# A two-block network on one core: another order of the expert units with late products last, and less GpSimd arithmetic behind the experts

## The chip, the cores and the metric

The kernel runs on one core of a Trainium2 chip. The metric is the device time of one execution in microseconds (us); less is better. The core has five engines that run their own instruction streams in order and meet at semaphores: PE (TensorE, the matmuls), DVE (VectorE), ACT (ScalarE), POOL (GpSimd) and SP (SyncE, which here only issues DMAs). DMAs are also issued from POOL's stream.

## The reference, cut to what matters

Everything is float32; `x` is 512 tokens of 1024 values, `c` one row of 1024.

```python
# block 1: a mixer, then 4 of 32 experts for each token
h = rmsnorm(x, norm2_w) * (1 + scale2) + shift2
gates = softmax(top4(h @ w_router + b_router))
hu = h[rows of e] @ w_up[e] + b_up[e]              # 1024 -> 2 x 1024
glu, lin = minimum(hu[:, :1024], 7), clip(hu[:, 1024:], -7, 7)
y = (glu * sigmoid(1.702 * glu) * (lin + 1)) @ w_down[e] + b_down[e]
x = x + gate2 * (sum over the 4 experts of gates * y)
# block 2: four sublayers: windowed attention, MLP, recurrent block, MLP
shift, scale, gate = split(silu(c) @ ada_w[i, s] + ada_b[i, s])
x = layer_norm(sqrt2 * x + (1 + gate) * f(x * (1 + scale) + shift), ln_g, ln_b)
```

An expert's weights are 8 MB for the up half and 4 MB for the down half; all 32 experts are read, 384 MB.

## The kernel before, in words

**Expert stage** (about 430 to 1528 us of the span). Experts are ranked by their number of tokens, and the table `UNITS` (L37-48) lays the ranks out as 20 blocks of 128 rows in 10 units: `_single(a)` is a block that one expert fills, `_pair(a, b, n)` one that two experts share. A unit is a list of steps, a step a list of blocks (mostly one). For every unit the tokens of its blocks are gathered by matmuls with one-hot columns (`gather_T`, L1145; `gather_unit` always makes 256 columns). For every step `expert_up` runs the up half (`bank_hu`, 8 tiles of 1 MB for each expert), then `expert_down` runs the down half of the step **before** it (`bank_y`, 4 tiles for each expert), and `transposed` (L1203) turns the new activations round. All products go through `products` (L1134). `pin` holds PE to the order in which the code is written. Rank 2 and on are known only on the chip: SP loads the expert's number into a register (L1277) before it can issue that expert's weights.

The weights come through a ring of 13 buffers of 1 MB, filled by SP in the order of use (L301); a load waits for its buffer. After unit 1 (`LOOP`) stands a loop for overflowing experts, which makes no trip on this input.

The result of a block is scaled by its tokens' gates on ACT (`expert_out`) and scattered by an indirect DMA of POOL (L1226) to `y_d` in DRAM, which has four slots for each token. In the last unit, behind its first step, `expert_bias` adds the bias term, and `add_slots` (L1447-1459) reads the four slots of all tokens back: 16 loads of 512 KB issued by POOL (L1456) into three pairs of buffers, each pair added, multiplied by `g2bc` (the second gate, spread over the partitions) and added to `x` on DVE. The last two blocks never go through `y_d`: `late_add` scales them (L1246), splits them in a high and a low part (L1247, L1248), multiplies both by the transposed one-hot rows `hotT` on PE (L1251, L1252) and adds the bank to `x` on DVE (L1253). The first late block's `late_add` stands ahead of the transposes and of the last down half in PE's order.

**Stages behind the experts** (1528 to 2862 us). Matmuls are made of three passes over parts that are split in high and low (`mm3`, L319-321); the weights come as 512 KB tiles and are split by ACT (`wh`, L310) and by DVE or POOL (`wl`, L315 or L313). `add_y` multiplies a result by the gate (L1618, DVE) and adds it to `x` (L1619, mostly POOL). `stats` and `normalise` (L1625-1633, DVE) make the layer norm, with small 128x1 steps for the root (L326-338); `make_hT` transposes `x` on PE (L1596), and ACT and DVE split it (`h_hi`, `h_lo`, L1603). `affine` (L1643, L1644, POOL) then multiplies `x` by `ln_g` and adds `ln_b`, for the residual. The modulation rows come from `c` times `ada_w`: three of them inside attention, `ada(1, ...)`, by `gemv_split`: for each of 8 tiles a multiply and add over 128x1024 on ACT, DVE (L389) or POOL (L392) into `gacc`, and 4 matmuls at the end (L395). `behind(3)` places instructions behind the last `h_hi` and `h_lo` of `make_hT`.

Of the kernel before, what the change touches and what calls it, by code (L numbers as in the profile page):

```python
# [256 lines left out]
def tile_block(ctx, tc, A, out, dbg=None):  # L257
# [118 lines left out]
    def gemv_split(src, cofs, gp, ring_raw, nv=4):  # L376

        acc = gp.tile([128, 1024], F, tag="gacc", name="gacc", bufs=1)
        for k in range(KD):
            if ring_raw:  # L380
                r = raw(src[k])
            else:
                r = gp.tile([128, 1024], F, tag="graw", name="graw", bufs=2)
# [721 lines left out]
    hot0 = [hot_cols(Z[:, :, 64 + b], hot_of(b, (b, 0, 128, 0))) for b in range(2)]  # L1105
# [46 lines left out]
    def gather_unit():  # L1152
        return gather_T([hots[-1][:, tb] for tb in range(NTB)], 256)
# [76 lines left out]
    def late_rows(b):  # L1230

        hotT = mt([128, 1024], "ma", 3, FR, mo)[:, 0:512]
        pt = trbank()
        for tb in range(NTB):
            pin(pe.matmul(out=pt[:, tbs[tb]], lhsT=hots[-1][:, tb, 128 * b:128 * b + 128].bitcast(F), rhs=ident,
                          start=True, stop=True))
        act.copy(out=hotT, in_=pt)
        return hotT

    def late_add(y, gc, hotT):  # L1240

        yh, yl = (mt([128, 8, 128], "aT", 3, FR, mo).rearrange("p a b -> p (a b)") for _ in range(2))
        t_ = mt([128, 1024], "yb", 2, F, mo)
        for h in range(2):
# [3 lines left out]
            vec.tensor_tensor(out=yl[:, hs], in0=t_[:, hs], in1=yh.bitcast(F)[:, hs], op=OP.subtract)  # L1248
            for tb in range(NTB):
                o = pbank("hu")  # L1250
                pin(pe.matmul(out=o, lhsT=hotT[:, tbs[tb]], rhs=yh[:, hs], start=True, stop=False))  # L1251
                pin(pe.matmul(out=o, lhsT=hotT[:, tbs[tb]], rhs=yl[:, hs], start=False, stop=True))  # L1252
                vec.tensor_tensor(out=xs[tb][:, hs], in0=o, in1=xs[tb][:, hs], op=OP.add)  # L1253
# [193 lines left out]
    def add_slots():  # L1447

        spare = mt([128, 8, 256], "xT", 2).rearrange("p a b -> p (a b)")
        pairs_ = [[h2_("l", 0), h2_("l", 1)], [h2_("l", 2), h2_("l", 3)], [spare[:, 0:1024], spare[:, 1024:2048]]]  # L1450
        for tb in range(NTB):
            for j in (0, 2):
                y = pairs_[0]
                pairs_.append(pairs_.pop(0))
                for i, t in enumerate(y):
                    pool.dma_start(out=t, in_=y_d[(j + i) * T + tb * 128:(j + i) * T + tb * 128 + 128, :])  # L1456
                vec.tensor_tensor(out=y[0], in0=y[0], in1=y[1], op=OP.add)
# [579 lines left out]
```

## Time and profile before

| | before |
|---|---|
| median of 3 runs | 2861.84 us (2855.33 to 2865.29) |
| profiled execution | 2863.78 us, span 2861.8 us |
| mean granted TensorE clock | 0.96 |
| PE, DVE, ACT, POOL busy | 92%, 50%, 27%, 17% of the span |
| DMA | 647.34 MB, mean 226 GB/s |
| slices 9 to 20 of 40 (572 to 1431 us) | 370 to 422 GB/s |
| chain that ended last | PE 46%, DMA 15%, DVE 12%, ACT 2% |

The times of the profile count from the span's start. A row of a group of instructions ends with the idle time of its engine just before them and what ended most of it; a row of a timeline has that in brackets. In a row of windows the DMA share can stand a little above 1.

### The profile page before, as it was taken

The page shows a single profiled execution, that of the slowest core. Times are in us where ns is not written, and L with a number is a line of the kernel's source. Part 1 is how long each engine was busy: PE and PEld are TensorE (multiplying, and loading weights), DVE is VectorE, ACT ScalarE, POOL GpSimd, SP SyncE. Part 2 cuts the span into 40 slices and gives each one's busy share as a digit, 9 for nine tenths or more (in the row PEclk, how much of TensorE's full clock was granted, in tenths as well). Part 3 has the DMA queues.
Part 4 walks back from the last instruction along what each step waited for, and adds up shares of the span by engine and source line. Part 5 has one row for each costly group of instructions (what it writes and reads, how often), then busy time and mean ns, then how long its engine had stood idle before and what let it go on. Part 6 is the DMA issues. An engine that isn't in the chain of part 4 may idle for free.

```text
span 2861.8 us, 37210 instructions
## 1 busy us (share of the span) xinstructions
PE 2620.6 (92%) x14592; PEld 1705.2 (60%) x14592; DVE 1419.4 (50%) x2470; ACT 766.5 (27%) x1312; POOL 483.3 (17%) x371
## 2 busy tenths in 40 slices
PE   7999998988999999999948898999988898799997
PEld 4777774433445334334315567777867677688886
DVE  4865573211112111111254668676478888855456
ACT  4432430000000100001004444232235555333231
POOL 1000000000000000000013213333251334422223
PEclk9999998999999999999978998999999899799999
DMA  7355457799999999999983424564323222232231
GB/s 269 111 178 185 149 184 291 306 421 389 421 421 372 422 421 421 421 421 370 421 346 130 157 81 151 175 225 150 98 77 105 72 86 86 70 107 95 89 103 52
DMA packets 128241, 647.34 MB, mean 226 GB/s; under 512 B 16272, under 2 KB 17252, under 8 KB 78912
## 3 DMA queue, kind: packets, MB, share of 16 engines
q1 hardware_dynamic: 121936, 628.07, 57.9%
q0 software_dynamic: 5984, 16.35, 1.5%
q8 instruction: 116, 1.90, 0.3%
q14 instruction: 61, 0.50, 0.1%
q10 hardware_dynamic: 144, 0.52, 0.0%
HBM read 624.42 MB, written 22.12 MB: 226 GB/s over the span
## 4 chain that ended last, share of the span: by engine, by line
PE 46%; DMA 15%; DVE 12%; ACT 2%; issue 2%; POOL 0%; DVEq 0%; SPq 0%; ACTq 0%
PE bank_hu L1134 11%; DMA raw<-in_w_up_dram 6%; PE bank_y L1134 5%; PE bank_d L319 5%; PE bank_d L321 4%; PE bank_d L320 4%; DMA raw<-in_w_down_dram 4%; PE bank_u L321 3%; PE bank_u L319 3%; PE bank_u L320 3%; DVE wl L315 2%; DMA graw<-in_ada_w_dram 2%; PE bank_tr L1145 2%; DMA raw<-in_ada_w_dram 1%; DVE vv L1951 1%
## 5 line engine op out<-in xcount | busy, mean ns | idle before, releaser
L1134 PE MATMUL bank_hu<-raw,xT 128*32 128x512 f32 (+2 forms) x3456 | 573.5, 598 | 13.7 <-DMA raw<-in_w_up_dram 13.7
L1134 PEld LDWEIGHTS bank_hu<-raw,xT 128*32 128x32 f32 (+2 forms) x3456 | 203.2, 124 | 363.1 <-issue 323.6
L315 DVE TENSOR_TENSOR wl<-raw,wh 128x1024 fp32r<-128x1024 f32 (+1 forms) x222 | 315.7, 1431 | 124.7 <-ACT wh L310 123.1
L310 ACT CAST wh<-raw 128x1024 fp32r<-128x1024 f32 (+1 forms) x231 | 236.6, 1042 | 442.6 <-PE bank_u L320 169.9
L1619 POOL TENSOR_TENSOR h2h<-h2h,yt 128x512 f32<-128x512 f32 x161 | 238.2, 1487 | 686.3 <-DVE yt L1618 676.4
L1134 PE MATMUL bank_y<-raw,aT 128*32 128x512 f32 (+2 forms) x1536 | 259.7, 596 | 8.9 <-DMA raw<-in_w_down_dram 8.8
L1191 DVE TENSOR_SCALAR ma<-bank_hu 128x256 f32<-128x256 f32 x80 | 34.0, 425 | 468.2 <-PE bank_hu L1134 468.2
L319 PE MATMUL bank_u<-h_hi,wh 128*128 128x512 f32 (+1 forms) x680 | 253.7, 375 | 5.9 <-ACT h_hi L1603 3.1
L321 PE MATMUL bank_u<-h_hi,wl 128*128 128x512 f32 (+1 forms) x680 | 253.0, 373 | 6.2 <-DVE wl L315 6.2
L320 PE MATMUL bank_u<-h_lo,wh 128*128 128x512 f32 (+1 forms) x680 | 252.6, 372 | 5.8 <-DVE h_lo L1603 5.8
L319 PE MATMUL bank_d<-wh,a 128*128 128x512 f32 x512 | 202.5, 396 | 5.7 <-DVE yt L1618 3.4
L1618 DVE TENSOR_TENSOR yt<-bank_d,G 128x512 f32<-128x512 f32 x168 | 113.2, 686 | 182.9 <-PE bank_d L321 177.2
L320 PE MATMUL bank_d<-wl,a 128*128 128x512 f32 x512 | 200.6, 392 | 0.0
L1192 ACT ACTIVATE mb<-ma 128x256 f32<-128x256 f32 x80 | 33.3, 417 | 619.0 <-DVE ma L1191 612.9
L321 PE MATMUL bank_d<-wh,b 128*128 128x512 f32 x512 | 197.7, 393 | 0.0
L1134 PEld LDWEIGHTS bank_y<-raw,aT 128*32 128x32 f32 (+2 forms) x1536 | 84.3, 124 | 173.2 <-issue 155.4
L1226 POOL DMA_INDIRECT y_d<-yb,ii x18 | 17.7, 984 | 921.0 <-ACT yb L1223 689.7
L321 PEld LDWEIGHTS bank_u<-h_hi,wl 128*128 128x128 f32 x680 | 132.2, 195 | 29.3 <-DVE wl L315 7.0
L320 PEld LDWEIGHTS bank_u<-h_lo,wh 128*128 128x128 f32 x680 | 132.4, 195 | 28.3 <-DVE h_lo L1603 6.4
L319 PEld LDWEIGHTS bank_u<-h_hi,wh 128*128 128x128 f32 x680 | 132.3, 196 | 27.8 <-ACT h_hi L1603 3.3
L1204 DVE COPY aT<-bank_tr 128x512 f32<-128x512 f32 x20 | 13.8, 691 | 246.2 <-PE bank_tr L1203 246.2
L319 PEld LDWEIGHTS bank_d<-wh,a 128*128 128x128 f32 x512 | 96.4, 188 | 31.1 <-DVE yt L1618 5.6
(556 smaller groups left out, 4264.0 us busy)
## 6 DMA issues: line engine op xcount, KB each, us to landing
raw<-in_w_up_dram SPq DMA_DIRECT2D x256, 1024.0 KB, 19.3
raw<-in_w_down_dram SPq DMA_DIRECT2D x128, 1024.0 KB, 19.8
raw<-in_mlp_w_dram SPq DMA_DIRECT2D x128, 512.0 KB, 4.4
graw<-in_ada_w_dram SPq DMA_DIRECT2D x72, 512.0 KB, 4.1
graw<-in_w_ada_dram SPq DMA_DIRECT2D x48, 512.0 KB, 4.7
raw<-in_ada_w_dram SPq DMA_DIRECT2D x24, 512.0 KB, 3.6
raw<-in_rnn_w_in_dram SPq DMA_DIRECT2D x24, 512.0 KB, 4.0
raw<-in_w_in_dram SPq DMA_DIRECT2D x22, 512.0 KB, 4.0
```

The source lines that it names most:

```text
L310: act.copy(out=h, in_=r)
L315: vec.tensor_tensor(out=l, in0=r, in1=h.bitcast(F), op=OP.subtract)
L319: pe.matmul(out=o, lhsT=lhs[0], rhs=rhs[0], start=first, stop=False)
L320: pe.matmul(out=o, lhsT=lhs[0], rhs=rhs[1], start=False, stop=False)
L321: pe.matmul(out=o, lhsT=lhs[1], rhs=rhs[0], start=False, stop=last)
L1134: pin(pe.matmul(out=o[at + a:at + a + tile], lhsT=lhs[:, a:a + tile], rhs=rhs, start=start, stop=stop, tile_position=(0, at + a)))
L1145: pin(pe.matmul(out=pt[:, j * n:j * n + n], rhs=hot[tb], lhsT=h2s[part][tb][:, (k + j) * 128:(k + j + 1) * 128], start=part + tb == 0, sto ...
L1191: vec.tensor_scalar(out=a, in0=hu[:, 0:256], scalar1=7.0, scalar2=None, op0=OP.min)
L1192: act.activation(out=b, in_=a, func=AF.Tanh, scale=0.851)
L1618: vec.tensor_tensor(out=t, in0=ps, in1=G[:, cs], op=OP.mult)
L1619: eng.tensor_tensor(out=xs[tb][:, cs], in0=xs[tb][:, cs], in1=t, op=OP.add)
L1951: vec.tensor_tensor_scan(out=v[:, r], data0=aa[:, o, r], data1=v[:, r], initial=0.0, op0=OP.mult, op1=OP.add)
```

## The change

There are two parts.

1. **Expert stage.** `UNITS` has 11 units of the same 20 blocks: the first is the single block of rank 0, whose gather makes 128 columns and whose down half runs at once; the others are mixed anew. `expert_out` scales on DVE, by the gate and by `g2bc` at once, so `add_slots` no longer multiplies. `add_slots` is cut in two: slots 0 to 3 at its old place, 4 to 7 placed behind the first late block's split. The products of both late blocks stand behind the last down half, and share their banks: one add on DVE for both.
2. **Behind the experts.** The 9 `wl` splits of L313, `affine`, the factor `SQRT2`, the 24 multiplies by `qq` in the recurrent block (L1950) and 21 of the 161 POOL adds of `add_y` go to DVE; 140 of these adds stay on POOL. The three rows of `ada(1, ...)` are made by `gemv_ring`: 32 matmuls each, with `c` spread over 32 columns (`rep`), no `gacc`.

```diff
 UNITS = [
-    [_single(0), _single(1)],
+    [_single(0)],
     [_pair(7, 25, 96), _pair(8, 26, 96)],
-    [_pair(15, 16, 64), _single(4)],
-    [_pair(9, 27, 96), _pair(17, 18, 64)],
+    [_single(1), _pair(15, 16, 64)],
+    [_pair(9, 27, 96), _single(4)],
+    [_pair(17, 18, 64), _pair(10, 28, 96)],
     [[[(2, 0, 128, 0)], [(2, 0, 64, 128), (14, 64, 64, 0)]]],
-    [_pair(10, 28, 96), _pair(19, 20, 64)],
-    [_pair(11, 29, 96), _single(5)],
-    [_pair(12, 30, 96), _pair(21, 22, 64)],
+    [_pair(19, 20, 64), _pair(11, 29, 96)],
+    [_single(5), _pair(12, 30, 96)],
+    [_pair(21, 22, 64)],
     [[[(3, 0, 128, 0)], [(6, 0, 96, 0), (3, 96, 32, 128)]]],
     [_pair(23, 24, 64), _pair(13, 31, 96)],
 ]
...
+    def gemv_ring(src, rep):
+        ps = bank("g")
+        for k in range(KD):
+            r = raw(src[k])
+            for q in range(4):
+                pe.matmul(out=ps[32 * q:32 * q + 32, 0:256], lhsT=rep[:, k, :], rhs=r[:, q * 256:q * 256 + 256],
+                          start=k == 0, stop=k == KD - 1, tile_position=(0, 32 * q))
+        return ps[:, 0:256]
...
-            act.activation(out=yb[:, n * 512:n * 512 + 512], in_=y[n], func=AF.Copy, scale=sl[1])
+            vec.scalar_tensor_tensor(out=yb[:, hs], in0=y[n], scalar=sl[1], in1=g2bc[:, hs], op0=OP.mult, op1=OP.mult)
...
                     if late:
-                        late_add(y, sl[1], hotT)
+                        with tc.issue_after(added.ins):
+                            parts = [late_parts(y, sl[1], "aT")]
+                        with tc.issue_after(parts[0][2].ins):
+                            add_slots(range(4, 8))
...
+            if u == 0:
+                for y, sl in zip(expert_down(*prev[:2]), prev[2]):
+                    expert_out(y, sl)()
+                prev = None
             if not nxt and n == 0:
                 expert_bias()
-                add_slots()
+                added = add_slots(range(4))
...
-    hotT = late_rows(1)
-    late_add(expert_down(*prev[:2])[0], prev[2][0][1], hotT)
+    y = expert_down(*prev[:2])[0]
+    os = [pbank("hu") for tb in range(NTB)]
+    late_products(os, hotT[0], parts[0], 0, True)
+    parts.append(late_parts(y, prev[2][0][1], "ma"))
...
-        for tb in range(NTB):
-            pool.tensor_tensor(out=xs[tb], in0=xs[tb], in1=g_, op=OP.mult)
-            pool.tensor_tensor(out=xs[tb], in0=xs[tb], in1=b_, op=OP.add)
+        with behind(3):
+            for tb in range(NTB):
+                vec.tensor_tensor(out=xs[tb], in0=xs[tb], in1=g_, op=OP.mult)
+                vec.tensor_tensor(out=xs[tb], in0=xs[tb], in1=b_, op=OP.add)
...
-                pool.tensor_tensor(out=v, in0=v, in1=qq[:, o, :], op=OP.mult)
+                vec.tensor_tensor(out=v, in0=v, in1=qq[:, o, :], op=OP.mult)
```

PE's order at the end of the expert stage, before (`bank_y` is a down half, `bank_hu` with `aT,ma` a late product, `bank_tr` a transpose, `bank_t` the first work of attention; the pair L1251, L1252 comes 8 times in each place):

```order
L1134 MATMUL bank_hu<-raw,xT 32x512 x45
L1235 MATMUL bank_tr<-ident,hot 128x128 x4
L1134 MATMUL bank_y<-raw,aT 64x512 x32
L1251 MATMUL bank_hu<-aT,ma 128x512
L1252 MATMUL bank_hu<-aT,ma 128x512
...
L1203 MATMUL bank_tr<-ident,ma 128x128 x8
L1235 MATMUL bank_tr<-ident,hot 128x128 x4
L1134 MATMUL bank_y<-raw,aT 32x512 x64
L1251 MATMUL bank_hu<-aT,ma 128x512
L1252 MATMUL bank_hu<-aT,ma 128x512
...
L1596 MATMUL bank_t<-ident,h2h_9680 128x128 x8
```

The same place with the change (line numbers are higher: 1134 is 1145, 1203 is 1214, 1596 is 1631, 315 is 316, 1643 is 1679):

```order
L1145 MATMUL bank_hu<-raw,xT 32x512 x48
L1246 MATMUL bank_tr<-ident,hot 128x128 x8
L1145 MATMUL bank_y<-raw,aT 64x512 x32
L1214 MATMUL bank_tr<-ident,ma 128x128 x8
L1145 MATMUL bank_y<-raw,aT 32x512 x64
L1266 MATMUL bank_hu<-aT,ma 128x512 x8
L1266 MATMUL bank_hu<-ma 128x512 x8
L1266 MATMUL bank_hu<-aT,ma 128x512 x8
L1266 MATMUL bank_hu<-ma 128x512 x8
L1631 MATMUL bank_t<-ident,h2h_9754 128x128 x8
```

The 16 late products that stood between the two down halves are gone from there; the transposes follow the first down half directly, and all 32 late products stand behind the second.

DVE's order in the boundary between attention and the first MLP, before (`h2h` is a tile of `x`; `affine` is not in it, since POOL has it):

```order
L1633 TENSOR_SCALAR h2h_9683<-h2h_9683,mv,lr 128x512 x2
L1603 TENSOR_TENSOR h_lo<-hf,h_hi 128x4x128 x4
L315 TENSOR_TENSOR wl<-raw,wh 128x1024 x2
L1603 TENSOR_TENSOR h_lo<-hf,h_hi 128x4x128 x2
L315 TENSOR_TENSOR wl<-raw,wh 128x1024 x3
```

The same place with the change:

```order
L1668 TENSOR_SCALAR h2h_9757<-h2h_9757,mv,lr 128x512 x2
L1638 TENSOR_TENSOR h_lo<-hf,h_hi 128x4x128 x4
L316 TENSOR_TENSOR wl<-raw,wh 128x1024 x2
L1638 TENSOR_TENSOR h_lo<-hf,h_hi 128x4x128 x2
L1679 TENSOR_TENSOR h2h_9754<-h2h_9754,lng 128x1024
L1679 TENSOR_TENSOR h2h_9755<-h2h_9755,lng 128x1024
L1679 TENSOR_TENSOR h2h_9756<-h2h_9756,lng 128x1024
L1679 TENSOR_TENSOR h2h_9757<-h2h_9757,lng 128x1024
L316 TENSOR_TENSOR wl<-raw,wh 128x1024 x2
L1680 TENSOR_TENSOR h2h_9754<-h2h_9754,lnb 128x1024
```

The multiplies by `ln_g` now stand on DVE behind the last `h_lo` and ahead of the next weight splits.

## Rows read from the trace of the kernel before

**Rows 1.** Time windows of the expert stage and one behind; the first line names the columns.
```profile
core 0: us, PE busy (x) PEld busy (x) DVE busy (x) ACT busy (x) POOL busy (x), PEclk, DMA share, GB/s
480.00:560.00 80.00, 79.38 (x451) 37.79 (x453) 17.12 (x44) 6.51 (x13) 1.09 (x1) 1.00 0.74 273
860.00:940.00 80.00, 78.43 (x452) 40.77 (x450) 17.23 (x48) 6.95 (x14) 0.97 (x1) 1.00 0.92 376
940.00:1300.00 360.00, 343.96 (x2432) 135.38 (x2428) 62.09 (x162) 27.69 (x54) 6.80 (x7) 1.00 1.01 421
1300.00:1360.00 60.00, 58.80 (x412) 28.75 (x406) 10.66 (x24) 6.63 (x12) 3.84 (x3) 1.00 0.93 361
1460.00:1510.00 50.00, 14.00 (x58) 7.61 (x58) 36.15 (x37) 2.41 (x4) 5.30 (x10) 0.62 0.63 252
2150.00:2490.00 340.00, 293.07 (x1246) 234.28 (x1245) 282.72 (x365) 177.10 (x250) 119.54 (x82) 0.92 0.26 83
```

**Rows 2.** DMA issues of the page: tile, queue, count, size, median us to landing.
```profile
raw<-in_w_up_dram SPq DMA_DIRECT2D x256, 1024.0 KB, 19.3
raw<-in_w_down_dram SPq DMA_DIRECT2D x128, 1024.0 KB, 19.8
```

**Rows 3.** Timeline of PE at the end of the expert stage: start, us, operation, idle before.
```profile
1459.54 2.74 PE L1134 MATMUL bank_y<-raw,aT 128*64 128x512 f32 x10
...
1474.65 0.77 PE L1251 MATMUL bank_hu<-aT,ma 128*128 128x512 f32 x1 [9.05 <-DVE h2h L1253]
...
1508.54 13.94 PE L1134 MATMUL bank_y<-raw,aT 128*32 128x512 f32 x128
...
1527.72 1.03 PE L1596 MATMUL bank_t<-ident,h2h 128*128 128x128 f32 x8
```

**Rows 4.** Groups of DVE from 1460 to 1510: busy, mean ns, idle before and its releaser.
```profile
L1457 DVE TENSOR_TENSOR h2l<-h2l,h2l 128x1024 f32<-128x1024 f32 x6 | 7.3, 1219 | 7.7 <-DMA h2l<-y_d 7.7
```

**Rows 5.** DMA issues from 1440 to 1500.
```profile
raw<-in_w_down_dram SPq DMA_DIRECT2D x6, 1024.0 KB, 22.8
```

**Rows 6.** Timeline of SP from 1440 to 1500.
```profile
1442.47 16.57 SPq L301 DMA_DIRECT2D raw<-in_w_down_dram  x6
```

**Rows 7.** Timeline of POOL from 1420 to 1500: the last read of `y_d`.
```profile
1492.93 0.53 POOL L1456 DMA_DIRECT2D h2l<-y_d  x1 [3.47 <-DVE h2h L1459]
```

**Rows 8.** Line 315, all its instructions: ns min/median/max.
```profile
L315 DVE TENSOR_TENSOR wl<-raw,wh x222: 1080/1225/3398, 40.7 to 2818.7; 128x1024 fp32r<-128x1024 f32 x103, 128x896 fp32r<-128x896 f32 x8
```

**Rows 9.** Groups of DVE by shape behind the experts.
```profile
L1619 DVE TENSOR_TENSOR h2h<-h2h,yt 128x512 f32<-128x512 f32 x7 | 4.8, 682 | 0.0
...
L389 DVE SCALAR_TENSOR_TENSOR gacc<-raw,sc,gacc 128x1024 f32<-128x1024 f32 x12 | 15.4, 1283 | 11.2 <-DMA raw<-in_ada_w_dram 9.6 <-ACT gacc L387 1.6
```

**Rows 10.** Groups of POOL behind the experts.
```profile
L1619 POOL TENSOR_TENSOR h2h<-h2h,yt 128x512 f32<-128x512 f32 x161 | 238.2, 1487 | 686.3 <-DVE yt L1618 676.4 <-DVE rs_x L331 3.7 <-DVE lr L338 3.3
...
L1950 POOL TENSOR_TENSOR vv<-vv,spare 128x512 f32<-128x512 f32 x24 | 47.8, 2026 | 5.9 <-ACT spare L1946 5.9
...
L1643 POOL TENSOR_TENSOR h2h<-h2h,lng 128x1024 f32<-128x1024 f32 x12 | 30.6, 2563 | 34.3 <-DMA lng<-ln_d 10.5 <-DVE lr L338 9.7 <-DVE rs_t L334 9.1
```

**Rows 11.** Timeline of DVE in the boundary behind the first MLP.
```profile
2123.82 0.22 DVE L334 SCALAR_TENSOR_TENSOR rs_t<-lr,rs_x 128x1 f32<-128x1 f32 x1
...
2126.78 2.34 DVE L334 SCALAR_TENSOR_TENSOR rs_t<-lr,rs_x 128x1 f32<-128x1 f32 x1
```

**Rows 12.** Timeline of POOL in the same boundary.
```profile
2126.57 4.88 POOL L1643 TENSOR_TENSOR h2h<-h2h,lng 128x1024 f32<-128x1024 f32 x2 [10.51 <-DMA lng<-ln_d]
```

**Rows 13.** Waits of PE behind the experts: releaser, us in total, times, longest.
```profile
PE bank_t L1596 <- DVE h2h L1633: 18.3, 3, 7.7
...
PE bank_t L1596 <- ACT hf L1600: 11.4, 6, 5.8
...
PE bank_u L321 <- DVE wl L315: 6.2, 2, 3.7
```

**Rows 14.** Timeline of PE in block 1: 16 row products of the form that `gemv_ring` adds.
```profile
204.17 1.21 PE L372 MATMUL bank_o<-graw,scb 128*32 128x256 f32 x16
```

More of the change, by code (lines that the diff above doesn't have):

```diff
@@ L1104, in tile_block @@
     hot_unit()
-    hot0 = [hot_cols(Z[:, :, 64 + b], hot_of(b, (b, 0, 128, 0))) for b in range(2)]
+    hot0 = hot_cols(Z[:, :, 64], hot_of(0, (0, 0, 128, 0)))
     sel0 = mt([128, 2], "sel0", 1, FR)
@@ L1150, in gather_T, with gather_unit @@
         return X
-    def gather_unit():
-        return gather_T([hots[-1][:, tb] for tb in range(NTB)], 256)
+    def gather_unit(n):
+        return gather_T([hots[-1][:, tb, 0:128 * n] for tb in range(NTB)], 128 * n)
     def products(o, rows, k, ws, start, stop):
@@ L1247, in late_add, with late_products @@
             act.copy(out=yh[:, hs], in_=t_[:, hs])
-            vec.tensor_tensor(out=yl[:, hs], in0=t_[:, hs], in1=yh.bitcast(F)[:, hs], op=OP.subtract)
-            for tb in range(NTB):
[L1250 to L1253, printed above, removed]
+            done = vec.tensor_tensor(out=yl[:, hs], in0=t_[:, hs], in1=yh.bitcast(F)[:, hs], op=OP.subtract)
+        return yh, yl, done
+    def late_products(os, hotT, parts, h, start):
+        for tb in range(NTB):
+            for i in range(2):
+                pin(pe.matmul(out=os[tb], lhsT=hotT[:, tbs[tb]], rhs=parts[i][:, h * 512:h * 512 + 512],
+                              start=start and i == 0, stop=not start and i == 1))
     def expert_w(ex):
@@ L1445, in expert_bias, with add_slots @@
             vec.tensor_tensor(out=xs[tb], in0=xs[tb], in1=bt, op=OP.add)
[L1447 to L1457, printed above, removed]
-                vec.tensor_tensor(out=y[0], in0=y[0], in1=g2bc, op=OP.mult)
-                vec.tensor_tensor(out=xs[tb], in0=xs[tb], in1=y[0], op=OP.add)
+    y_pairs = []
+    def add_slots(js):
+        if not y_pairs:
+            spare = mt([128, 8, 256], "xT", 2).rearrange("p a b -> p (a b)")
+            y_pairs.extend([[h2_("l", 0), h2_("l", 1)], [h2_("l", 2), h2_("l", 3)],
+                            [spare[:, 0:1024], spare[:, 1024:2048]]])
+        for j in js:
+            tb, y = j // 2, y_pairs[0]
+            y_pairs.append(y_pairs.pop(0))
+            for i, t in enumerate(y):
+                o = (2 * (j % 2) + i) * T + tb * 128
+                pool.dma_start(out=t, in_=y_d[o:o + 128, :])
+            vec.tensor_tensor(out=y[0], in0=y[0], in1=y[1], op=OP.add)
+            done = vec.tensor_tensor(out=xs[tb], in0=xs[tb], in1=y[0], op=OP.add)
+        return done
     LOOP = 1
@@ L1480, in tile_block @@
             if late:
-                hotT = late_rows(n - 1)
+                hotTs = mt([128, 1024], "ma", 3, FR, mo)
+                hotT = [late_rows(b) for b in range(2)]
             if prev is not None:
@@ L1518, in tile_block @@
             finish()
-    hotT = late_rows(1)
-    late_add(expert_down(*prev[:2])[0], prev[2][0][1], hotT)
+    y = expert_down(*prev[:2])[0]
+    os = [pbank("hu") for tb in range(NTB)]
+    late_products(os, hotT[0], parts[0], 0, True)
+    parts.append(late_parts(y, prev[2][0][1], "ma"))
+    for h in range(2):
+        if h:
+            os = [pbank("hu") for tb in range(NTB)]
+            late_products(os, hotT[0], parts[0], 1, True)
+        late_products(os, hotT[1], parts[1], h, False)
+        for tb in range(NTB):
+            cs = slice(h * 512, h * 512 + 512)
+            vec.tensor_tensor(out=xs[tb][:, cs], in0=os[tb], in1=xs[tb][:, cs], op=OP.add)
     mo.release()
@@ L1549, in tile_block @@
     first += load_first(3)
-    first[:] = [split(r, eng) for r, eng in zip(first, (None, pool, None))]
-    first += [split(r, pool) for r in load_first(1)]
+    first[:] = [split(r) for r in first]
+    first += [split(r) for r in load_first(1)]
     c2 = pc.tile([128, _NCOLS2], F, name="c2")
@@ L1784, in prepare @@
     def prepare(src, n):
-        early[:] = [weights(quarter(src, k), pool) for k in range(n)]
+        early[:] = [weights(quarter(src, k)) for k in range(n)]
     def starting(src, n):
@@ L1806, in down_group @@
                         k == 0, k == nk - 1)
-                add_y(w, tb, half, ps, G, vec if then is not None and tb == NTB - 1 else pool)
+                add_y(w, tb, half, ps, G, vec if then is not None else pool)
     def cols_mm(ps, hl, hT, ts):
@@ L1985, in tile_block @@
     hT = make_hT(mc[:, 0, 1, :], mc[:, 0, 0, :], False)
-    for tb in range(NTB):
-        pool.tensor_scalar(out=xs[tb], in0=xs[tb], scalar1=SQRT2, scalar2=None, op0=OP.mult)
+    with behind(3):
+        for tb in range(NTB):
+            vec.tensor_scalar(out=xs[tb], in0=xs[tb], scalar1=SQRT2, scalar2=None, op0=OP.mult)
     for s in range(4):
```

45 lines of the change are left out of this document (23 added, 22 removed).

## The prediction

> **What bounds the kernel now.** I read the page's slices first, then windows by stage, then the timelines where PE stands idle. The program has two halves with different bounds, and the two parts of the change fall one into each.
>
> In the expert stage the bound is the stream of weights. From 940 to 1300 us the DMAs move 421 GB/s at a share of 1.01, so nothing more fits in, while DVE works 62 of 360 us [rows 1]. The reader is to see that PE is called busy for 344 of these 360 us too; but a busy PE is not one at its peak, and what sets the pace is read from the transfer: 256 and 128 tiles of 1 MB [rows 2] at 421 GB/s are 384 x 1.0486 / 0.421 = 956 us, most of the stage's 1090. What lies above the 956 is time in which the stream stands still, and there are two kinds of it. Within the stage the rate is 273 GB/s from 480 to 560 us, 376 from 860 to 940 and 361 from 1300 to 1360 [rows 1]: 80 x (1 - 273/421) + 80 x (1 - 376/421) + 60 x (1 - 361/421) = 28 + 9 + 9 = 46 us lost. The other kind is the end. PE finishes a down half at 1459.54 + 2.74 = 1462.28 and begins the last one at 1508.54 [rows 3]: 46 us, with 14.00 of 50 us of work in that window and a clock of 0.62 [rows 1]. SP issued the last weight tile at the end of a run from 1442.47 of 16.57 us, so by 1459.04 [rows 6], and tiles issued there took 22.8 us [rows 5]: all weights lay in the chip by about 1482. So for some 26 us of the 46 the last down half waits for nothing that it needs. What it waits for is PE's order: the late products stand ahead of it, each bank of theirs waits for DVE's add (9.05 us at 1474.65, released by L1253) [rows 3], and DVE, in order, is held by the reads of `y_d` (7.7 us idle on DMA, then 1219 ns for each add) [rows 4], the last of which is issued at 1492.93 [rows 7].
>
> Behind the experts PE waits in short pieces, many of them around the boundaries of sublayers: 18.3 us for `normalise`, longest 7.7, 11.4 for the ACT step of `make_hT`, and 6.2 for a weight split [rows 13]. There DVE is slowed by POOL: the 128x1 root step takes 0.22 us, but 2.34 us [rows 11] once POOL has begun the affine of the same boundary at 2126.57 [rows 12]. Four or five such steps and a normalise lie in a chain, and PE's next transpose waits for its end.
>
> **Part 1, the end of the expert stage.** With the change the transposes and the last down half follow the first one directly. The last down half is then held by its weights. These were there at 1482; in the new order the second half of the `y_d` reads no longer waits for DVE's place behind the late products, so 8 loads of 512 KB may compete with weights: 4.2 MB at 421 GB/s is 10 us at most, but from 1460 to 1510 only 252 of 421 GB/s were used [rows 1], that is 20 us of free rate; I take 0 and keep 10 as the bound. After the last tile a quarter of the half remains, 13.94 / 4 = 3.5 us [rows 3]. So the last down half ends near 1485 instead of 1508.54 + 13.94 = 1522.48: 37 us. Behind it the new chain (scale, split, products of two blocks in one bank, adds) is longer than the old one, which took 1527.72 - 1522.48 = 5.2 us; I add 3, four or five adds of 0.68 us [rows 9]. The term is **-34 us**, bounds -24 and -40.
>
> **Part 1, the order of the units.** A single block takes 12 MB for the same PE time for which a pair takes 24 MB. Pairs and singles in turn, and a first block whose down half runs at once, return the ring's buffers earlier. The most this can give is the 46 us lost above; part of them cannot go, since the two units with two blocks in one step, around which the 9 + 9 lie, are still there, SP's wait for the experts' numbers comes now after 12 tiles instead of 13, the loop after unit 1 still cuts the stream, and there is one gather more (11 for 10). I take a quarter of the 28 + 9 + 9 us, **-10 us**, bounds 0 and -20. The two terms do not simply add: whatever the stream gains moves the last weight, and with it the end, so they do, as long as the weights are last there. If they are not, the reads of `y_d` are, and I take 4 us off: **-40** for the stage.
>
> Moving `expert_out` to DVE costs nothing: two operations for each of 18 scattered blocks, some 0.7 us each [rows 9], in a stage where DVE is free for five sixths [rows 1]. If that cover failed it would be 25 us over 1090.
>
> **Part 2, the work that DVE gets.** Prices from undisturbed rows: a split is 1.22 us [rows 8], a 512-wide add or multiply of two SBUF tiles 0.68 us [rows 9]; the 1024-wide affine I take like the adds in the tail, 1.22 us [rows 4]. So 9 splits are 11 us, 24 affine steps 29, four factors of SQRT2 at most 5, 24 multiplies by `qq` 16, 21 adds 14: 75 us more on DVE. Gone from it are 12 steps of `gacc`, 15.4 us [rows 9], and the slowing. POOL loses 12 affine steps at 2563 ns and as many for the other line (62 us), 24 multiplies at 2026 (49), 21 adds at 1487 (31) [rows 10] and 9 splits, at the affine's price 23: some 165 us of work beside DVE. A disturbed DVE step took up to 2 us more than an undisturbed one [rows 8, 11], so the slowing that goes with them lies between 0 and those 165 us; I take the middle, some 80. So DVE's total hardly changes, and the gain lies where its chain is what PE waits for.
>
> There I take the sum piece by piece: 12 of the 18.3 us for `normalise`, since the affine now stands behind the last `h_lo`; 4 of the 11.4 at `make_hT`, where the first splits leave POOL; 3 of 6.2 for splits, because the affine's 4 x 1.22 us stands ahead of the next ones [rows 4, 13]; 6 us at the ends of the sublayers and in the recurrent block, where an add or a multiply of 0.68 takes the place of 1.5 or 2.0 us [rows 9, 10]. That is 25. Against it: the three ring products, 96 matmuls, in place of 12. Sixteen of them took 1.21 us [rows 14], so 7 us on PE, part of it in idle time, plus waits if a tile of `ada_w` comes late, since these matmuls stand in PE's order: +5, bounds 0 and +12. The term is **-20 us**, bounds -35 and +8.
>
> **Sum**, against the profiled execution (2863.78 us, span 2861.8, 2 us above the median of the runs): -40 - 20 = -60, so 2863.8 - 60 = 2803.8, and 2802 against the median.
>
> **Rivals.** *The end stays half bound* (0.15): the reads of `y_d` and the last weights share the rate, or DVE's second half of the adds, which stands ahead of the last block's split, comes late. For it: the last read was issued only at 1492.93 [rows 7] and three pairs of buffers serve 8 pairs of loads. Against it: half of the adds now stand on DVE ahead of the first late block's scaling, beside the last up half. The gain at the end is then 14 instead of 34: 2822.
>
> *The change does not reach the disturbance* (0.13): 140 of the 161 POOL adds stay, by far the largest group of POOL's work (238.2 us, [rows 10]), so most weight splits are slowed as before, and part 2 gives 0 to 5: about 2820.
>
> *DVE becomes the bound behind the experts* (0.06, the slower side): in the recurrent block it works 282.72 of 340 us [rows 1], and the change gives it 75 us more, in order, ahead of weight splits. If the slowing by POOL does not fall, 75 - 15 = 60 us land on DVE; from 40 + 8.6 = 49 us of them in front of PE the kernel is slower, and with all 60 it is 2802 + 20 + 60 = 2882. Against it: in the boundary it is POOL's affine that stretches DVE, and that goes. A page of the Trainium skill speaks for this rival: "Perfetto Trace Analysis", section "Optimizing Scalar/DVE Operations", says that where DVE is saturated some of its work may go to other engines, even to GpSimd, though the two share a port of SBUF, so that it might not help; by that rule the move in the recurrent block goes the wrong way and costs about the 16 us of its multiplies there, while the trace speaks for the reservation: 0.22 us became 2.34 beside POOL's affine [rows 11, 12].
>
> *Both halves come short* (0.04): the end gives 10, the order costs 10 by a starved first unit, part 2 nothing: within 0.3% of 2862.
>
> **How the numbers follow.** A measurement of this kernel can tell some 0.3%, 8.6 us. The forecast, -60 with its bounds, has 0.62, and 2802 is its time. Faster by more than 0.3%: 0.62 + 0.15 + 0.13 = 0.90; same 0.04; slower 0.06. The range that should hold it 8 times in 10 runs from 2802 - 32 = 2770 (both halves near their better bounds) to 2838 (either of the first two rivals with some of the other); the two last rivals and a little at each end are left out.
>
> **What would show it.** In the profile of the changed kernel: no PE gap of tens of microseconds between the two last down halves, and a last one released by a weight tile; attention's first transpose near 1488 (1527.72 - 40); a rate above 273 GB/s from 480 to 560 us; 128x1 steps at 0.2 us in the boundaries, and no PE wait for `normalise` above 4 us. It is wrong if the time between the two last down halves stays above 30 us, if the stage's stream stands still longer than before, or if PE waits for `wl` or for the ring products by more than 15 us behind the experts.

## The result, and the profile after

| | before | after |
|---|---|---|
| median | 2862.66 us (2855.33 to 2865.29, 4 runs) | 2815.24 us (2809.15 to 2818.94, 4 runs) |
| profiled execution, span | 2863.78, 2861.8 us | 2809.15, 2807.3 us |
| PE, DVE, ACT, POOL busy | 92%, 50%, 27%, 17% | 94%, 49%, 26%, 10% |

The ratio is 0.9824, 95% interval 0.9804 to 0.9844: 47 us by the medians, where 60 were forecast. The changed kernel's profiled execution is the fastest of its four, so the 54.5 us between the two spans flatter it. By the ratio the gain is 50 us, 45 to 56.

The spans can be cut at four marks, the first transpose of `x` in each sublayer behind the experts. Before they stand at 1527.7, 1723.5, 2112.7 and 2464.0 us, after at 1498.7, 1697.7, 2086.6 and 2425.3. So 29.0 us came from everything up to the end of the expert stage; attention took 199.0 for 195.8, the first MLP 388.9 for 389.2, the recurrent block 338.7 for 351.3, and the rest 382.0 for 397.8: 25.5 us together behind the experts.

The windows of the changed kernel (answering to [rows 1]; the one from 940 holds what stood at 860 before):

```profile
core 0: us, PE busy (x) PEld busy (x) DVE busy (x) ACT busy (x) POOL busy (x), PEclk, DMA share, GB/s
480.00:560.00 80.00, 77.40 (x534) 32.99 (x532) 17.82 (x40) 5.16 (x11) 1.08 (x1) 1.00 0.81 321
860.00:940.00 80.00, 75.06 (x472) 30.42 (x464) 15.65 (x40) 4.68 (x10) 0.97 (x1) 1.00 1.01 421
940.00:1300.00 360.00, 354.13 (x2450) 148.80 (x2454) 75.77 (x187) 20.03 (x43) 6.82 (x7) 1.00 0.99 409
1300.00:1360.00 60.00, 59.76 (x400) 28.45 (x392) 14.58 (x30) 5.79 (x11) 3.83 (x3) 1.00 0.93 361
1460.00:1510.00 50.00, 32.66 (x190) 13.69 (x186) 27.08 (x33) 11.93 (x20) 3.30 (x7) 0.90 0.82 320
```

From 480 to 560 the rate rose from 273 to 321 GB/s and from 860 to 940 from 376 to 421. But 940 to 1300 fell from 421 to 409: the hole moved with its unit and did not go. In the window of the stage's end PE works 32.66 us where it worked 14.00. Over the whole recurrent block, from mark to mark, first before, then after:

```profile
2112.71:2463.97 351.26, 307.33 (x1330) 247.07 (x1329) 291.77 (x374) 183.75 (x263) 126.65 (x91) 0.93 0.26 82
```

```profile
2086.63:2425.34 338.71, 295.94 (x1317) 239.79 (x1316) 274.65 (x413) 185.53 (x263) 39.76 (x48) 0.94 0.27 86
```

DVE is busy 274.65 us there where it was 291.77, although it has taken work over.

In the kernel before, three more waits stand between the two last down halves beside the 9.05 us of [rows 3], all of a late product for DVE's add:

```profile
1491.56 0.79 PE L1251 MATMUL bank_hu<-aT,ma 128*128 128x512 f32 x1 [15.72 <-DVE h2h L1253]
...
1499.57 0.80 PE L1251 MATMUL bank_hu<-aT,ma 128*128 128x512 f32 x1 [6.79 <-DVE h2h L1253]
...
1504.29 0.79 PE L1251 MATMUL bank_hu<-aT,ma 128*128 128x512 f32 x1 [3.51 <-DVE h2h L1253]
```

Together the four are 35 of the 46 us. PE's timeline at the stage's end in the changed kernel (answering to [rows 3]):

```profile
1461.39 1.09 PE L1214 MATMUL bank_tr<-ident,ma 128*128 128x128 f32 x8
...
1465.35 4.79 PE L1145 MATMUL bank_y<-raw,aT 128*32 128x512 f32 x32 [0.86 <-DMA raw<-in_w_down_dram]
...
1472.85 5.34 PE L1145 MATMUL bank_y<-raw,aT 128*32 128x512 f32 x32 [2.71 <-DMA raw<-in_w_down_dram]
...
1480.36 4.80 PE L1145 MATMUL bank_y<-raw,aT 128*32 128x512 f32 x32 [2.17 <-DMA raw<-in_w_down_dram]
...
1487.62 3.62 PE L1145 MATMUL bank_y<-raw,aT 128*32 128x512 f32 x26 [2.46 <-DMA raw<-in_w_down_dram]
...
1498.73 1.09 PE L1631 MATMUL bank_t<-ident,h2h 128*128 128x128 f32 x8
...
1507.43 1.11 PE L1631 MATMUL bank_t<-ident,h2h 128*128 128x128 f32 x4 [7.61 <-ACT hf L1635]
```

The first down half ends and the transposes follow at 1461.39; no late product stands between. The last down half is now released by its weight tiles, as forecast, at 1465.35, 1472.85, 1480.36 and 1487.62: one pair of 1 MB tiles in 7.5 us, though 2.1 MB at the 421 GB/s of [rows 1] take 5.0. The half ends at 1491.24, not at 1485, and not 10 us before that, as with the gain from the order. Attention's first transposes come 7.5 us later, at 1498.73 (forecast: near 1488), and then PE idles for 7.61 us until ACT delivers `hf`.

PE's waits behind the experts, the largest of after (answering to [rows 13]):

```profile
PE bank_t L1631 <- ACT hf L1635: 15.1, 10, 7.6
...
PE bank_d L320 <- DVE gg L1957: 15.1, 2, 12.3
PE bank_r L320 <- ACT xh L1941: 13.1, 4, 9.8
PE bank_t L1631 <- DVE h2h L1668: 6.6, 2, 4.0
...
PE bank_d L321 <- DVE wl L316: 1.3, 2, 0.8
```

The wait for `normalise` fell from 18.3 to 6.6 us. The 6.2 us for weight splits at `bank_u` are gone, and at `bank_d` 1.3 of 1.8 are left. The wait for ACT's `hf` rose from 11.4 to 15.1 and that for `xh` in the recurrent block from 9.4 to 13.1; the one for `gg` there was 16.8 before. Two pieces of DVE in the boundary of [rows 11] show why the first fell:

```profile
2097.43 0.22 DVE L335 SCALAR_TENSOR_TENSOR rs_t<-lr,rs_x 128x1 f32<-128x1 f32 x1
...
2107.30 4.62 DVE L1679 TENSOR_TENSOR h2h<-h2h,lng 128x1024 f32<-128x1024 f32 x4
```

No 128x1 step in front of these normalises takes more than 0.22 us, and the affine (four steps, 4.62 us) now follows on DVE when the transposes have had what they need. But DVE and POOL still meet elsewhere, as the page's groups tell, first before, then after:

```profile
L315 DVE TENSOR_TENSOR wl<-raw,wh 128x1024 fp32r<-128x1024 f32 (+1 forms) x222 | 315.7, 1431 | 124.7 <-ACT wh L310 123.1 <-PE bank_u L321 0.7
```

```profile
L316 DVE TENSOR_TENSOR wl<-raw,wh 128x1024 fp32r<-128x1024 f32 (+1 forms) x231 | 306.4, 1334 | 131.6 <-ACT wh L311 128.9
...
L1654 POOL TENSOR_TENSOR h2h<-h2h,yt 128x512 f32<-128x512 f32 x140 | 211.2, 1514 | 765.5 <-DVE yt L1653 765.5
```

The splits' mean went from 1431 to 1334 ns, against 1.22 us undisturbed [rows 8]: about half of the slowing stayed, with the 140 adds.

### The profile page after: what moved, and what is told of

The parts are those of the page before. It is cut to its first block, busy times and chain, and to the rows that moved or that the text cites. A ratio compares the mean times of both kernels' runs of the same rounds, so it can differ in the third digit from the quotient of the medians.

```text
span 2807.3 us, 37551 instructions
## 1 busy us (share of the span) xinstructions
PE 2631.3 (94%) x14824; PEld 1705.6 (61%) x14824; DVE 1388.0 (49%) x2563; ACT 733.1 (26%) x1266; POOL 289.1 (10%) x280
## 4 chain that ended last, share of the span: by engine, by line
PE 54%; DMA 12%; DVE 8%; ACT 2%; issue 2%; POOL 0%; DVEq 0%; SPq 0%; ACTq 0%
PE bank_hu L1145 14%; PE bank_y L1145 6%; PE bank_d L320 6%; PE bank_d L321 6%; PE bank_d L322 6%; DMA raw<-in_w_up_dram 4%; DMA raw<-in_w_down_dram 4%; PE bank_u L320 3%; PE bank_u L322 3%; PE bank_u L321 3%; PE bank_tr L1156 2%; DMA graw<-in_ada_w_dram 2%; DVE wl L316 2%; DMA raw<-in_mlp_w_dram 1%; DVE vv L1989 1%
## 5 line engine op out<-in xcount | busy, mean ns | idle before, releaser
L1145 PEld LDWEIGHTS bank_hu<-raw,xT 128*32 128x32 f32 (+2 forms) x3456 | 196.4, 123 | 360.4 <-issue 338.2
L316 DVE TENSOR_TENSOR wl<-raw,wh 128x1024 fp32r<-128x1024 f32 (+1 forms) x231 | 306.4, 1334 | 131.6 <-ACT wh L311 128.9
L1654 POOL TENSOR_TENSOR h2h<-h2h,yt 128x512 f32<-128x512 f32 x140 | 211.2, 1514 | 765.5 <-DVE yt L1653 765.5
L1145 PE MATMUL bank_y<-raw,aT 128*32 128x512 f32 (+2 forms) x1536 | 264.4, 601 | 18.6 <-DMA raw<-in_w_down_dram 17.2
L1235 DVE SCALAR_TENSOR_TENSOR yb<-bank_y,gc,g2bc 128x512 f32<-128x512 f32 x32 | 24.0, 751 | 208.1 <-PE bank_y L1145 206.2
```

The costliest lines, as they stand in the source:

```text
L316: vec.tensor_tensor(out=l, in0=r, in1=h.bitcast(F), op=OP.subtract)
L1145: pin(pe.matmul(out=o[at + a:at + a + tile], lhsT=lhs[:, a:a + tile], rhs=rhs, start=start, stop=stop, tile_position=(0, at + a)))
L1654: eng.tensor_tensor(out=xs[tb][:, cs], in0=xs[tb][:, cs], in1=t, op=OP.add)
```

## The experiments

Each ratio is to the kernel before, run on the same chip; us are worked out from it with the 2863 us of the kernel before, where no median is named. A difference from the changed kernel is taken from its 0.9824. Measured again it gave 0.9835 (below), by which each gain over it would be 3 us larger and each loss 3 us smaller.

**The new order of units alone.** `UNITS`, `hot0`, `gather_unit(n)` and the down half at `u == 0`, nothing else.

```diff
-    [_single(0), _single(1)],
+    [_single(0)],
...
+            if u == 0:
+                for y, sl in zip(expert_down(*prev[:2]), prev[2]):
+                    expert_out(y, sl)()
+                prev = None
```

> The kernel before with the new order of units alone (11 units, the first with one block, its gather 128 wide, its down half at once); late products, add_slots and all stages behind the experts as before. Theory A (the stream of weights gains little from the order: in the changed kernel tile 370 to 380 was issued only 3 to 4 us earlier than before, and it loses 9 to 10 us again at each of the two units with two blocks in one step): -3 to -6 us against the kernel before. Rival B (the order carries the third of the gain that I gave it): -10 us or more. Rival C (the order pays only with the new end): 0, because the end of the stage is held by the late products and reads, which have their own time.

Measured 0.9989 (0.9978 to 1.0000): -3 us, between 0 and -6. The middle is theory A's; rival B falls. Rival C, no gain at all, is at the edge of the interval. This kernel's first mark lies 4.0 us earlier (1523.7 for 1527.7), which speaks against it, but one profile of this stage is not good to 4 us (last section), so C is not excluded. Its windows, with [rows 1] beside them:

```profile
480.00:560.00 80.00, 77.39 (x558) 33.77 (x561) 18.27 (x46) 6.95 (x14) 1.09 (x1) 1.00 0.81 323
560.00:620.00 60.00, 47.81 (x349) 21.54 (x342) 9.13 (x24) 4.28 (x8) 0.99 (x1) 0.89 0.93 380
860.00:940.00 80.00, 74.87 (x498) 31.38 (x498) 15.51 (x44) 5.95 (x12) 0.97 (x1) 1.00 1.01 421
940.00:1300.00 360.00, 353.96 (x2408) 148.38 (x2407) 63.68 (x166) 29.01 (x57) 6.78 (x7) 0.99 0.98 407
1300.00:1360.00 60.00, 59.73 (x400) 28.44 (x394) 13.52 (x28) 7.06 (x13) 3.83 (x3) 1.00 0.92 358
```

The loss against 421 GB/s from 480 to 560 is 18.6 us instead of 28.1, but 560 to 620, where nothing was lost before (422 GB/s), loses 5.8 (the loop's hole has moved there from 620 to 700, which ran at 391 GB/s and lost 5.7), 940 to 1300 loses 12 where 860 to 940 lost 8.6, and 1300 to 1360 still 9. In sum 45 us against 51 from 480 on, and 2 more lost at the start (261 GB/s from 400 to 480 for 271): about 4 us gained.

**The new end alone.** `expert_out`, `add_slots` in two halves, `late_parts`, `late_products`.

```diff
-                        late_add(y, sl[1], hotT)
+                            parts = [late_parts(y, sl[1], "aT")]
...
+    late_products(os, hotT[0], parts[0], 0, True)
```

> The kernel before with the new end of the expert stage alone (expert_out on DVE with the second gate, reads of y_d in two halves, late products of both blocks behind the last down half); units in their old order, behind the experts as before. Theory A (the end is nearly all of the stage's gain, and is now bound by the last weight tile and the reads beside it): -25 to -30 us. Rival B (the end needs the new order to pay): -15 us or less. Rival C (the shorter adds and the scaling on DVE do it, not the order on PE): then the gap between the two last down halves stays above 20 us; by A it falls below 12 us.

Measured 0.9906 (0.9883 to 0.9929): -27 us, within A. PE's timeline:

```profile
1463.42 1.09 PE L1203 MATMUL bank_tr<-ident,ma 128*128 128x128 f32 x8
...
1482.48 5.34 PE L1134 MATMUL bank_y<-raw,aT 128*32 128x512 f32 x32 [2.21 <-DMA raw<-in_w_down_dram]
...
1490.03 3.62 PE L1134 MATMUL bank_y<-raw,aT 128*32 128x512 f32 x26 [2.21 <-DMA raw<-in_w_down_dram]
```

The transposes follow the first down half at once, and the weight tiles come 7.55 us apart here too. The gap is gone. This run changes PE's order, the adds and the scaling together, and with the products moved no wait for them can stand there, so its sign can't tell rival C from A. For the order speak the 35 us of waits for the products shown above; shorter adds in the old order were not run.

**The moves to DVE behind the experts alone**, `gacc` kept.

```diff
-            pool.tensor_tensor(out=xs[tb], in0=xs[tb], in1=g_, op=OP.mult)
+                vec.tensor_tensor(out=xs[tb], in0=xs[tb], in1=g_, op=OP.mult)
...
-                pool.tensor_tensor(out=v, in0=v, in1=qq[:, o, :], op=OP.mult)
+                vec.tensor_tensor(out=v, in0=v, in1=qq[:, o, :], op=OP.mult)
```

> The kernel before with the moves from GpSimd to VectorE behind the experts alone (weight splits, affine, SQRT2 factor, multiplies by qq, 21 of the adds); gacc stays. Theory A (POOL's affine held DVE's chain at the boundaries): -20 to -28 us, most of it at the boundaries in front of the recurrent block and of the last MLP. Rival B (DVE becomes the bound): 0 or slower. Rival C (the gain behind the experts comes from the ring products, which take gacc off DVE): -10 us or less here.

Measured 0.9934 (0.9911 to 0.9956): -19 us, between -13 and -25: the middle lies just short of A's range, and the interval leaves both rivals out. By the marks the recurrent block took 342.2 us (351.3 before) and what follows it 382.9 (397.8); attention and the first MLP gained nothing. The two waits of PE are already those of the whole change:

```profile
PE bank_t L1596 <- ACT hf L1600: 15.6, 10, 7.5
...
PE bank_t L1596 <- DVE h2h L1633: 6.6, 2, 4.0
```

The rise of the wait for `hf` thus came with these moves and not with the new end, alone with which it is 9.8 us.

**The ring products alone.**

```diff
-        ada(1, 0, gacc, "ring")
+        ada(1, 0, rep, "ring")
```

> The kernel before with the ring products alone (96 matmuls in place of gacc inside attention). Theory A: +2 to +5 us, since 84 more matmuls stand in PE's order and idle time hides a part. Rival B: no change or faster, since DVE and POOL lose the gacc steps (12 of 1.28 us on DVE, 9 of 2.4 us on POOL) and attention's own steps run undisturbed: -2 to -6 us.

Measured 0.9997 (0.9985 to 1.0009): no change, from -4 to +3 us. Both theories' nearer ends lie in that interval, and it can't say more than that the extra matmuls cost little and bring little. The four parts give -27 - 3 - 19 - 1 = -50 us; the whole measured -50 by its ratio (-45 to -56). They add, within what these runs can tell.

**No second half of the reads.** The reads of `y_d` for tokens 256 to 511 and their adds are left out. (The numbers 0 to 7 in `add_slots` count pairs of reads, two for each 128 tokens, and not the four slots of a token.)

```diff
-                            add_slots(range(4, 8))
+                            pass
```

> The changed kernel without the second half of add_slots: the reads of slots of tokens 256 to 511 from y_d (8 loads, 4.2 MB) and their adds are left out. Theory A (the end of the stage is the end of one full stream, into which the reads are mixed: pairs of weight tiles came 7.5 us apart where 2.1 MB take 5 us): the last down half ends 8 to 10 us earlier, the whole -8 to -10 us against the changed kernel. Rival B (the reads cost nothing, since there is rate to spare, as I forecast): -2 us or less. Rival C (DVE's adds hold the second late block): the pairs of weight tiles still come 7 us apart, and the gain comes behind the last down half.

Measured 0.9790 (0.9775 to 0.9806), 10 us below the changed kernel's 0.9824. PE's timeline at the end:

```profile
1473.70 3.64 PE L1145 MATMUL bank_y<-raw,aT 128*32 128x512 f32 x32 [1.33 <-DMA raw<-in_w_down_dram]
...
1478.64 3.62 PE L1145 MATMUL bank_y<-raw,aT 128*32 128x512 f32 x26 [1.30 <-DMA raw<-in_w_down_dram]
...
1482.19 2.12 PE L1266 MATMUL bank_hu<-aT,ma 128*128 128x512 f32 x8
```

The last pairs come 4.94 us apart where they came 7.5 apart, and the last down half ends at 1482.26, 9.0 us earlier. A single profile can be off by 8 us at this mark, but from the transposes between the two last down halves to the end of the second it takes 20.4 us here and 26.8 to 30.3 in the seven profiles with the new end and the reads in their place. Theory A holds: 4.2 MB of reads in a full stream cost about the 10 us that they take at 421 GB/s. This is the bound that the prediction kept for them while it took 0. Where the free rate of the window from 1460 to 1510 lay shows when that window is cut, before:

```profile
1460.00:1482.00 22.00, 5.85 (x20) 2.46 (x16) 16.84 (x17) 1.24 (x2) 3.71 (x7) 0.74 1.01 418
1482.00:1510.00 28.00, 8.15 (x38) 5.15 (x42) 19.31 (x20) 1.17 (x2) 1.59 (x3) 0.54 0.34 122
```

and in the changed kernel up to its last pair of tiles:

```profile
1460.00:1487.00 27.00, 18.23 (x116) 4.64 (x112) 10.74 (x12) 1.73 (x3) 3.30 (x7) 0.94 1.02 415
```

**The affine back on POOL**, all else as changed.

```diff
-        with behind(3):
-            for tb in range(NTB):
-                vec.tensor_tensor(out=xs[tb], in0=xs[tb], in1=g_, op=OP.mult)
+        for tb in range(NTB):
+            pool.tensor_tensor(out=xs[tb], in0=xs[tb], in1=g_, op=OP.mult)
```

> The changed kernel with the affine back on GpSimd (24 steps of 1024 columns), all else as changed. Theory A (POOL's affine held the chain of small DVE steps and normalise in front of PE's transposes): +14 to +22 us against the changed kernel, PE's waits for normalise back at 15 to 18 us, 128x1 steps of 2 us in the boundaries. Rival B (the affine's place behind make_hT, not the engine, is what frees the chain, or splits and adds do it): +6 us or less.

Measured 0.9879 (0.9858 to 0.9900): 16 us above the changed kernel, give or take 8. That is A's range; by the second measurement it would be 13, and rival B's 6 would lie inside the interval. The trace decides for A: by the marks the recurrent block took 346.6 us (338.7 in the changed kernel) and the last MLP 390.5 (382.0), and the wait for `normalise` is back:

```profile
PE bank_t L1631 <- DVE h2h L1668: 18.5, 6, 7.6
```

and the 128x1 steps stretched again in the boundary in front of the recurrent block, where POOL began the affine at 2101.14 (two neighbours on DVE):

```profile
2101.05 0.22 DVE L335 SCALAR_TENSOR_TENSOR rs_t<-lr,rs_x 128x1 f32<-128x1 f32 x1
...
2101.31 2.24 DVE L339 SCALAR_TENSOR_TENSOR lr<-rs_t,lr 128x1 f32<-128x1 f32 x1
```

The affine thus carries most of the 19 us. This kernel changes engine and place together, so the share of each stays open.

**All of the adds on DVE.**

```diff
-                add_y(w, tb, half, ps, G, vec if then is not None else pool)
+                add_y(w, tb, half, ps, G, vec)
```

> The changed kernel with the 140 adds of add_y that stayed on GpSimd, and the 2 adds of the last store, on VectorE too. Theory A (what is left of the slowing, about 86 us of DVE time beside these adds, lies beside PE's work in the MLPs, off its path): -3 to +3 us. Rival B (DVE becomes the bound: 142 x 0.68 = 97 us more in its order): +8 us or more. Rival C (the slowed weight splits still hold PE): -8 us or more.

Measured 0.9792 (0.9778 to 0.9805), 9 us below the changed kernel: theory A falls and rival B with it, and the number is rival C's; 144 operations more (four in the last store, not two), 98 us in DVE's order, did no harm. By the marks the first MLP took 384.7 us, 4.2 less, and the recurrent block 336.8, 1.9 less. The splits lost their last slowing:

```profile
L316 DVE TENSOR_TENSOR wl<-raw,wh 128x1024 fp32r<-128x1024 f32 (+1 forms) x231 | 279.3, 1218 | 107.7 <-ACT wh L311 104.6
```

No single wait of PE names the gain: its idle time behind the experts is 3 us less (89.5 for 92.7), and PE hardly waits for splits in either kernel, so rival C's mechanism is not shown. The largest piece is the wait for `gacc` in the first MLP, 1.6 us where it was 3.7.

**The fourth split later.** In the changed kernel ACT, in order, waits for two weight tiles ahead of `hf`:

```profile
1501.02 1.05 ACT L311 CAST wh<-raw 128x1024 fp32r<-128x1024 f32 x1 [5.49 <-DMA raw<-in_attn_w_in_dram]
1504.93 1.04 ACT L311 CAST wh<-raw 128x1024 fp32r<-128x1024 f32 x1 [2.87 <-DMA raw<-in_attn_w_in_dram]
```

```diff
-    first += [split(r) for r in load_first(1)]
+    fourth = load_first(1)
...
+        with behind(0):
+            first.extend(split(r) for r in fourth)
         project(0, first)
```

> The changed kernel with one move at the start of attention: the split of the fourth weight tile stands behind the first block of make_hT on ACT and DVE, not ahead of it. In the changed kernel ACT waits 5.5 and 2.9 us for two weight tiles (loads issued at 1497.4) before it can begin hf, and PE stands idle for 7.6 us. Theory A: the transposes of the second half of tokens start 5 us earlier and the whole is 3 to 6 us faster. Rival B: PE then waits for the fourth tile instead: 0 to -2 us.

Measured 0.9814 (0.9801 to 0.9828), 3 us below the changed kernel's ratio, with intervals that overlap: theory A's nearer end, but the times alone don't part it from rival B. The trace is plainer:

```profile
1506.87 0.66 PE L1631 MATMUL bank_t<-ident,h2h 128*128 128x128 f32 x4 [1.07 <-ACT hf L1635]
```

The 7.61 us in front of the second transposes are 1.07 here, and attention took 192.3 us instead of 199.0.

**The changed kernel again, and both last moves together**, on one chip.

> The changed kernel once more, unaltered, beside the next two on the same chip: a measure of what the other differences are worth. Both theories: ratio 0.9804 to 0.9844 to the kernel before.

> The changed kernel with both moves: the 142 adds that stayed on GpSimd on VectorE, and the split of the fourth weight tile behind the first block of make_hT. Theory A (each frees another piece of PE's path: weight splits in the MLPs, the start of attention): -8 to -13 us against the changed kernel on the same chip. Rival B (the 9 us of the adds alone were a difference between chips): -3 to -5 us.

The changed kernel measured 0.9835 (0.9814 to 0.9855), 2816.04 us; with both moves 0.9785 (0.9771 to 0.9799), 2802.27 us: 13.8 us faster on the same chip, a little above theory A's range, and rival B falls. The first MLP took 386.0 us (390.0 in the changed kernel beside it), attention 191.7 (199.2). This version beats both kernels.

**The late reads behind the weights**, on top of that.

```diff
+                d_ = pool.dma_start(out=t, in_=y_d[o:o + 128, :])
+                tc.add_manual_dep(d_.ins, pinned[0].name, mybir.DependencyInfo(
+                    mybir.DependencyClass.Sync, mybir.DependencyReason.DATA), reason="late read")
```

> The kernel of r2 with the last 8 reads of y_d held back by a wait on the third quarter of the last down half, in four pairs of buffers, and their adds behind those of the late products. Theory A (the stream sets the end: the weights come 8 to 10 us earlier if the reads stand behind them, and the transposes of the first 256 tokens need none of these reads): the last down half ends 7 to 10 us earlier, attention's first transposes too, and 4 to 8 us of it are kept, since DVE now waits for the reads ahead of the first h_lo. Rival B (the reads are only moved to where PE waits for them): the last down half ends earlier, and the whole is -2 to +3 us against r2.

Measured 0.9785 (0.9770 to 0.9799), 2801.86 us: nothing against the kernel without it. PE's timeline, then DVE's, then ACT's:

```profile
1484.07 3.62 PE L1145 MATMUL bank_y<-raw,aT 128*32 128x512 f32 x26 [1.30 <-DMA raw<-in_w_down_dram]
...
1495.17 1.04 PE L1648 MATMUL bank_t<-ident,h2h 128*128 128x128 f32 x8
...
1508.65 0.80 PE L320 MATMUL bank_d<-wh,h_hi 128*128 128x512 f32 x1 [9.22 <-ACT h_hi L1655]
```

```profile
1497.52 1.21 DVE L1572 TENSOR_TENSOR h2l<-h2l,h2l 128x1024 f32<-128x1024 f32 x1
...
1506.60 1.22 DVE L1573 TENSOR_TENSOR h2h<-h2h,h2l 128x1024 f32<-128x1024 f32 x1
1507.85 1.23 DVE L1573 TENSOR_TENSOR h2h<-h2h,xT 128x1024 f32<-128x1024 f32 x1
...
1509.19 1.28 DVE L1655 TENSOR_TENSOR h_lo<-hf,h_hi 128x512 fp32r<-128x512 f32 x2
```

```profile
1507.98 1.14 ACT L1655 CAST h_hi<-hf 128x512 fp32r<-128x512 f32 x2 [9.27 <-DVE h2h L1573]
```

Attention's first transposes come at 1495.17, 8.3 us earlier than in the kernel beside it (1503.5), and the last pairs of tiles come 4.94 us apart, as without the reads. But the adds of the late reads (L1572, L1573) run on DVE from 1497.52 to 1509.08, and ACT's first `h_hi` waits 9.27 us for the last but one of them, the last that reads `h2l`, though it computes nothing from it; the first `h_lo` follows at 1509.19, and PE idles 9.22 us. Attention took 203.7 us instead of 191.7. Rival B holds: the wait only moved. That `h_hi` is laid over the `h2l` buffers of the reads, which come free with that add, would explain ACT's wait; it is inferred, and a kernel with the reads in other memory was not tried. The first `h_lo` stands behind all of these adds in DVE's order in any case.

## Why the prediction was right, and where it was off

The sign and the range held: 47 us against 60, 2815 in a range from 2770 to 2838, and none of the rivals came as a whole. So did the two main mechanisms, the late products in PE's order and POOL's affine in DVE's chain. The miss lies in the expert stage; that the term behind it fits so well is in part luck. By its steps:

- **The end of the stage, -34: measured -27** alone. That the late products in PE's order made the gap, and that weight tiles release the last down half afterwards, is shown by the two timelines; that the new end is worth this much, by the run with the end alone. The step that failed is "I take 0 and keep 10 as the bound" for the reads beside the weights. The free rate of 20 us in the window from 1460 to 1510 was counted there, but it lay behind 1482, when the last weight was due: up to there the stream ran at 418 GB/s before, and in the changed kernel at 415 up to the last tile. Leaving half of the reads out gave back about 9 us at that place. The sum would have been -24 for this term with the bound. The chain behind the last down half was sized well: 7.5 us in the changed kernel and in the run with the end alone, for 5.2 + 3.
- **The order of the units, -10: measured -3** (0 to -6). The failed step is "a quarter of the 28 + 9 + 9 us". Of the 28, 9.5 went, but the loop's hole stayed, and the loss at the first unit with two blocks in one step grew from 8.6 to 12 us. The prediction named both as things that cannot go, and left the loop's 5.7 us out of its sum.
- **The two add** to -30 within what the runs can tell, so nothing shows the 4 us taken off for overlap, and the stage gave -30, not -40. That is the miss of some 10 us.
- **Behind the experts, -20: measured -19 and -1.** The size was right, and some of its pieces were not. `normalise` gave 11.7 of its 18.3 us (12 forecast), the weight splits all of the 6.2 (3 forecast). ACT's `hf` was to give 4 of 11.4 and went up to 15.1; attention, where the first splits left POOL, became 3.2 us longer in the profiled runs. The run with the fourth split later shows what stands there: loads of weights in ACT's order ahead of `hf`. The ring products were to cost 5 and cost nothing that can be measured. These errors cancel, and that is the luck in the -20; the 6 us at the ends of the sublayers and in the recurrent block were not measured apart. DVE's total, which was hardly to change, fell from 1419 to 1388 us.
- **The rival of half an end** was partly true: the end is bound by reads and weights together, as it said, at a price of 10 us rather than 20.
- **The rival of the disturbance that stays** was true of the adds: taking the remaining ones off POOL gave about 9 us more, by a way that no wait names. It was wrong for the boundaries, where the affine was what held PE.
- **The rival of a DVE that becomes the bound** fell twice: with the change, and with 144 more operations on DVE. The Trainium skill's "Perfetto Trace Analysis", section "Optimizing Scalar/DVE Operations", had spoken for it, with the reservation of the shared port. The recurrent block, where DVE was busiest, took 12.6 us less in the profiled run with the work moved to DVE (10.1 in the second profile of the changed kernel), so here the reservation decides. Its ground stands in "SBUF — State Buffer", section "SBUF: two separate sides": a DVE operation with two SBUF inputs and a GpSimd operation that reads SBUF hold the pair of ports one at a time, each for its whole instruction. The trace agrees: 0.22 us became 2.34 beside a POOL step [rows 11, 12], and 2.24 again when the affine went back.

## What to carry to other kernels

Where a stream of weights sets the end of a stage, as here, a transfer put ahead of the last tile is paid in full (10 us for 4.2 MB), and free rate counts only if it lies ahead of that tile. An engine that looks idle enough to take work off another can cost more than it takes when both meet at the same memory: look at the smallest steps of the chain that PE waits for, and see what runs beside those that are ten times too long. A wait taken out in one place (the late reads) can stand up again in the next engine's order, so follow what is queued behind the moved work.

## What was not expected of the hardware

A weight split on DVE took 1431 ns on the mean in the kernel before, with 161 adds and the affine on POOL, 1334 in the changed one with 140 adds and no affine, and 1218 with neither: moving the last 140 adds onto the busier engine made the program faster by some 9 us. And two profiled executions of the same changed kernel reached the end of the expert stage at 1498.7 and 1506.7 us, so a single profile of this stage is good to about 8 us, and the -29.0 of the first comparison must be read with that.
